# Crowded experts: one loop over blocks of 32 slots in place of nested written-out blocks

## The chip, the cores and the metric

The kernel runs on one core of a Trainium2 chip. The metric is device time in microseconds of one execution, from a median of runs.

## The reference, cut to what matters

One layer: a token mixer (retention and an mLSTM side by side) and then a mixture of experts over 512 tokens with 1024 features. Each token goes to one of 4 groups and there to 2 of 8 experts, so 1024 assignments are spread over 32 experts. What an expert gets depends on the data.

```python
def expert_block(args):
    xb, e = args
    return (jax.nn.silu(xb @ w_e1[e]) * (xb @ w_e3[e])) @ w_e2[e]
...
xs = u[slot_tok].reshape(n_blocks, MOE_BLOCK, D)
ys = lax.map(expert_block, (xs, block_exp)).reshape(n_slots, D)
out = jnp.zeros((N, D), F32).at[slot_tok].add(slot_w[:, None] * ys)
```

The weights `w_e1` and `w_e3` are 1024 x 512 and `w_e2` 512 x 1024 in float32, so an expert has three matrices of 2 MB.

## The kernel before, in words

The stages ahead of the experts (modulation, projections, scans, branches, routing) take the first 995 us or so of the span and are not touched. The routing leaves, in SBUF, for each expert the number of blocks of 32 slots that it fills (`nblk`), a row in the output scratch `y_d` (`orow`), and for each token its rank in its expert (`rm`).

The experts run in order, in one written-out Python loop (32 copies of the code). The order of the instructions on TensorE is the order of the source there (a manual schedule); the other engines are ordered by the scheduler. Copies of the weights go through a ring of ten 2 MB slots; SyncE issues the three loads of a later expert after each expert's code (L936). For expert e:

- `nb = values_load` (L1561) reads the next expert's count into a register of every engine.
- `hidden_q` for slots 0 to 31: 64 matmuls of 32 slots by 256 columns (L1464), their gate on ScalarE and VectorE (`swiglu`, L1445 to L1447).
- If n >= 2 (L1567): the same for slots 32 to 63.
- Every fourth expert: `gather`, which picks the rows of the next four experts with one-hot matmuls (L1424).
- `output_q`: two transposes (L1454), their copy (L1456), the output product (L1475, 32 matmuls in the trace), a product with the gate on VectorE (L1477), and a store on ScalarE's queue.
- `slots_in`: VectorE copies the next expert's slots from PSUM to `xT` (L1432).
- If n >= 2 (L1577): output of the second block and its store (L1579). Inside it, if n > 2 (L1580): `several`, the crowded path.

`several` before: `more` builds the one-hot of 64 slots (`osb`, L1482, against `rme`, L1496), gathers them with 96 matmuls (L1488) and copies them, half on ScalarE (L1490), half on VectorE (L1491). `some` runs `hidden_q` and `output_q` for 32 of them and stores the result in four DMAs of 32 KB from GpSimd (L1505). `some(1, ...)` stands in its own If, n > 3 (L1509); then n > 4 (L1511) with a second `more`, n > 5 (L1514), n > 6 (L1516), and in that a loop for n from 6 on (L1518). For the two blocks of one `more` there are two halves of `yq`, and so the first product of the second block can run while the first block's result is stored.

Of the 32 experts, 21 have n of 0 or 1, 8 have n = 2, two (25 and 28) have n = 3 and one (24) has n = 5, as the branches in the trace show.

## Time and profile before

| what | us |
|---|---|
| median of three runs | 1705.09 |
| lowest and highest of them | 1703.87, 1715.65 |
| the profiled execution | 1702.87 |
| its span, first to last instruction | 1700.9 |

The profile is one execution taken by the hardware profiler. PE is TensorE's matmuls, PEld its weight loads, DVE is VectorE, ACT ScalarE, POOL GpSimd, SP SyncE; a q behind the name is the engine's sequencer, which runs branches, waits and register loads. A wait is idle time of an engine in front of an instruction, put down to what came last. PEclk is the granted clock of TensorE as a share of its full speed. Weights (LDWEIGHTS) and matmuls of one product are separate instructions. The rows that matter stand in the section on rows.

### The profile page before, as it was taken

What the parts mean: (1) busy time and instruction counts of PE and PEld (TensorE: products, weight loads), DVE (VectorE), ACT (ScalarE), POOL (GpSimd) and SP (SyncE); (2) the same over time, 40 slices, a digit from 0 to 9 for tenths busy, and PEclk for the clock granted to TensorE, in tenths of its full rate; (3) what the DMA queues carried; (4) which work ended last, traced back from release to release, by engine and by line L of the source; (5) the groups of instructions that cost most, each with busy time, mean ns of one, the idle gap of its engine ahead of it and who ended that gap; (6) DMA issues with size and microseconds to landing.
All of it is one profiled execution on the core that took longest, in us unless ns stands there. A gap on an engine that the chain in (4) does not pass through costs nothing. (4 is left out here: it accounts for less than half of the span.)

```text
span 1700.9 us, 29095 instructions
## 1 busy us (share of the span) xinstructions
PE 1405.3 (83%) x11759; PEld 1101.2 (65%) x11759; DVE 785.4 (46%) x1893; ACT 426.1 (25%) x768; POOL 184.6 (11%) x113
## 2 busy tenths in 40 slices
PE   5999898999999999999999656576657676777774
PEld 3888888888898989899887544243434343444431
DVE  7747386567546475657687951111111111111115
ACT  3422254334444444445341210000000000000001
POOL 0101063235000000000132420000000000000003
PEclk9999999999999999999999778788878887998987
DMA  9324964344322122214557758889797979447544
GB/s 350 118 77 148 304 194 145 106 143 137 82 69 69 51 83 67 69 56 149 184 176 267 297 215 334 319 346 392 305 354 285 355 295 394 189 164 286 212 167 152
DMA packets 155875, 344.63 MB, mean 203 GB/s; under 512 B 18152, under 2 KB 110712, under 8 KB 147396
## 3 DMA queue, kind: packets, MB, share of 16 engines
q1 hardware_dynamic: 147544, 328.38, 53.2%
q10 hardware_dynamic: 6252, 7.73, 1.4%
q0 software_dynamic: 1792, 4.85, 0.8%
q8 instruction: 160, 2.62, 0.6%
q14 instruction: 127, 1.04, 0.2%
HBM read 307.37 MB, written 33.57 MB: 200 GB/s over the span
## 5 line engine op out<-in xcount | busy, mean ns | idle before, releaser
L1464 PE MATMUL ps_h<-w,xT 128*32 128x256 f32 x3072 | 241.2, 479 | 143.8 <-PEq L1561 96.0
L1464 PEld LDWEIGHTS ps_h<-w,xT 128*32 128x32 f32 x3072 | 131.8, 136 | 253.3 <-issue 199.1
L1446 DVE SCALAR_TENSOR_TENSOR t<-t,ps_h 64x256 f32<-64x256 f32 x48 | 19.8, 413 | 293.2 <-ACT t L1445 293.1
L187 DVE TENSOR_TENSOR w_lo<-raw,w_hi 128x1024 fp32r<-128x1024 f32 x96 | 127.2, 1348 | 23.6 <-ACT w_hi L186 23.6
L1445 ACT ACTIVATE t<-ps_h 64x256 f32<-64x256 f32 x48 | 17.7, 376 | 455.7 <-PE ps_h L1464 440.1
L1475 PE MATMUL ps_y<-w,hT 128*32 128x256 f32 x1536 | 104.7, 418 | 19.6 <-ACT hT L1456 11.9
L186 ACT ACTIVATE w_hi<-raw 128x1024 fp32r<-128x1024 f32 x96 | 96.1, 1050 | 60.3 <-PE ps_t L207 18.0
L550 POOL TENSOR_TENSOR macc<-macc,mw 128x1024 f32<-128x1024 f32 x32 | 81.5, 2546 | 97.3 <-DMA macc<-in_b_ada_dram 48.6
L1432 DVE COPY xT<-xg 128x128 f32<-128x128 f32 (+1 forms) x120 | 30.0, 295 | 125.9 <-PE xg L1424 65.6
L1475 PEld LDWEIGHTS ps_y<-w,hT 128*32 128x32 f32 x1536 | 49.0, 117 | 55.9 <-ACT hT L1456 15.9
L1424 PE MATMUL xg<-sg,u 128*128 128x256 bf16 (+1 forms) x768 | 80.5, 266 | 2.1 <-PEq L1567 1.2
L206 PE MATMUL ps_q<-u_lat,w_hi 128*128 128x512 f32 x192 | 78.4, 408 | 2.4 <-ACT u_lat L312 1.7
L1424 PEld LDWEIGHTS <-u 128*128 128x128 bf16 x768 | 70.5, 98 | 13.8 <-issue 6.4
L207 PE MATMUL ps_q<-u_lat,w_hi 128*128 128x512 f32 x192 | 77.9, 406 | 0.2 <-DVE u_lat L313 0.2
L208 PE MATMUL ps_q<-u_lat,w_lo 128*128 128x512 f32 x192 | 77.8, 405 | 0.0
L1505 POOL DMA_DIRECT2D y_d<-yq x20 | 10.2, 510 | 613.3 <-DVE yq L1477 500.7
L206 PE MATMUL ps_g<-w_hi,u_lat 128*128 128x256 f32 x256 | 72.6, 284 | 0.0
L208 PE MATMUL ps_g<-w_hi,u_lat 128*128 128x256 f32 x256 | 72.6, 284 | 0.0
L207 PE MATMUL ps_g<-w_lo,u_lat 128*128 128x256 f32 x256 | 72.5, 283 | 0.0
L206 PE MATMUL ps_v<-w_hi,u_lat 128*128 128x256 f32 x256 | 72.1, 282 | 0.0
L207 PE MATMUL ps_v<-w_lo,u_lat 128*128 128x256 f32 x256 | 72.1, 282 | 0.0
L208 PE MATMUL ps_v<-w_hi,u_lat 128*128 128x256 f32 x256 | 72.1, 282 | 0.0
(394 smaller groups left out, 3384.6 us busy)
## 6 DMA issues: line engine op xcount, KB each, us to landing
w<-in_w_e_dram SPq DMA_DIRECT2D x96, 2048.0 KB
raw<-in_w_in_dram SPq DMA_DIRECT2D x40, 1024.0 KB
mw<-in_w_ada_dram SPq DMA_DIRECT2D x32, 512.0 KB
y_d<-plain SPq DMA_DIRECT2D x28, 512.0 KB
wada<-in_w_ada_dram SPq DMA_DIRECT2D x4, 2048.0 KB
y_d<-yt ACTq DMA_DIRECT2D x43, 128.0 KB
tanh_d<-tg SPq DMA_DIRECT2D x16, 256.0 KB
br_d<-rt SPq DMA_DIRECT2D x16, 256.0 KB
```

The source lines that it names most:

```text
L186: S.activation(h_, r_, AF.Copy)
L187: V.tensor_sub(l_, r_, f32(h_))
L206: PE.matmul(ps, lh, rh, start=first, stop=False)
L207: PE.matmul(ps, lh, rl, start=False, stop=False)
L208: PE.matmul(ps, ll, rh, start=False, stop=last)
L550: G.tensor_add(acc, acc, w)
L1424: PE.matmul(xg[j // step][:, j % step], u2[s_][:, i, j * P:(j + 1) * P], sg[:, i], start=(i == 0 and s_ == 0), stop=(i == 3 and s_ == 2))
L1432: V.tensor_copy(xT[:, j:j + step, :], xg[j // step][:, :, n, :])
L1445: S.activation(t, ps[0:64, 0:256], AF.Tanh, scale=0.5)
L1446: V.scalar_tensor_tensor(t, t, 1.0, ps[0:64, 0:256], op0=OP.add, op1=OP.mult)
L1464: PE.matmul(ps[32 * a:32 * a + 32, 0:256], x[:, kt, 32 * b:32 * b + 32], w[a // 2][:, kt, 256 * (a % 2):256 * (a % 2) + 256], start=(kt == ...
L1475: PE.matmul(py[32 * a:32 * a + 32, 0:256], hT[:, kt % 2, 32 * (kt // 2):32 * (kt // 2) + 32], w2[:, kt, 256 * a:256 * a + 256], start=(kt ...
```

## The change

`several` becomes one loop that runs once for each block of 32 slots from the third on: the offset of the ranks falls by 32, `more` gathers 32 slots in place of 64 into the first half of `xT` (VectorE alone copies), and one block runs and is stored. The nested Ifs, their copies of the block and the hidden loop behind them are gone; so are the two halves of `yq`.

```diff
-    rme = m1p.tile([P, 4, 2], F32, name="rme")
+    rme = m1p.tile([P, 4, 1], F32, name="rme")
...
-        S.copy(xT[:, 0:4], ps[:, 0:4])
-        V.tensor_copy(xT[:, 4:8], ps[:, 4:8])
+        V.tensor_copy(xT[:, :, 0:32], ps)
...
     def several(e, w, n, xT, yq):
 
-        for b in range(2):
-            V.tensor_scalar(rme[:, :, b:b + 1], rm[:, :, e:e + 1], -64.0 * (b + 1), None, op0=OP.add)
-
+        V.tensor_scalar(rme, rm[:, :, e:e + 1], -32.0, None, op0=OP.add)
         base = nc.values_load(orow[0:1, e:e + 1], min_val=64 * NE, max_val=64 * NE + 1024)
-
-        def some(b, row):
-
-            y = yq[:, b, :]
-            output_q(hidden_q(xT, w, b), w[2], y)
+        with tc.For_i(2, n) as i:
+            V.tensor_scalar(rme, rme, -32.0, None, op0=OP.add)
+            more(xT)
+            output_q(hidden_q(xT, w, 0, gated("t")), w[2], yq)
             for a in range(4):
-                stored(G.dma_start(y_d[bass.ds(row, 32), 256 * a:256 * a + 256], y[32 * a:32 * a + 32, :]))
-
-        more(0, xT)
-        some(0, base)
-        with tc.If(n > 3, label=f"more{e}d"):
-            some(1, base + 32)
-            with tc.If(n > 4):
-                more(1, xT)
-                some(0, base + 64)
-                with tc.If(n > 5):
-                    some(1, base + 96)
-                    with tc.If(n > 6):
-                        V.tensor_scalar(rme, rme, -64.0, None, op0=OP.add)
-                        with tc.For_i(6, n, 2) as i:
-                            V.tensor_scalar(rme, rme, -64.0, None, op0=OP.add)
-                            more(0, xT)
-                            for b in range(2):
-                                some(b, base + i * 32 - 64 + 32 * b)
+                stored(G.dma_start(y_d[bass.ds(base + i * 32 - 64, 32), 256 * a:256 * a + 256], yq[32 * a:32 * a + 32, :]))
```

The lines of the new kernel are some 22 lower: the first If of an expert is L1545, the second L1555, the crowded path's L1558, and the loop L1495.

On PE, in the code of expert 0 of before, the second block's output ends and the crowded path begins with its first `more` (`ps_or` is its PSUM tile, `u` one of the three parts of the tokens):

```order
5672 L1475 MATMUL ps_y<-w_10040,hT 32x256 x16
5673 L1577 COMPARE_AND_BRANCH
5674 L1454 MATMUL ps_ht<-small,t_10118 128x64 x2
5675 L1475 MATMUL ps_y<-w_10040,hT 32x256 x16
5676 L1580 COMPARE_AND_BRANCH
5677 L1488 LDWEIGHTS u_9126
```

In the new program the crowded path stands at the same place (row 5676), but other rows follow it, as below. This is where the crowded path of before ends, behind its inner loop, with the ends of the nested Ifs, and the next expert begins:

```order
6367 L1475 MATMUL ps_y<-w_10040,hT 32x256 x16
6368 L1518 REGISTER_ALU
6369 L1518 COMPARE_AND_BRANCH
6370 L1518 UNCONDITIONAL_BRANCH
6371 L1516 UNCONDITIONAL_BRANCH
6372 L1514 UNCONDITIONAL_BRANCH
6373 L1511 UNCONDITIONAL_BRANCH
6374 L1509 UNCONDITIONAL_BRANCH
6375 L1580 UNCONDITIONAL_BRANCH
6376 L1577 UNCONDITIONAL_BRANCH x2
6377 L1561 TENSOR_LOAD nblk
```

Rows 5677 to 6375 are what an expert with n = 2 jumps over. A float32 matmul of these rows is two weight loads and two matmuls on the engine, so these rows are 1796 instructions, and 1870 with the second block's output.

In the new program PE has at the same place the entry of the loop, with a compare of its own and a block of its own in front of the body:

```order
5672 L1474 MATMUL ps_y<-w_10040,hT 32x256 x16
5673 L1555 COMPARE_AND_BRANCH
5674 L1453 MATMUL ps_ht<-small,t_10118 128x64 x2
5675 L1474 MATMUL ps_y<-w_10040,hT 32x256 x16
5676 L1558 COMPARE_AND_BRANCH
5677 L1495 COMPARE_AND_BRANCH
5678 L1495 UNCONDITIONAL_BRANCH x2
5679 L1656 BRANCH_PREFETCH_HINT
5680 L1487 LDWEIGHTS u_9126
5681 L1487 MATMUL ps_or<-osb,u_9126 128x32
```

Three branch rows and a hint have come in front of the gather; the gather's matmuls are 32 columns wide. The end of the body, and of the crowded path, on PE in the new program; the next expert follows:

```order
5889 L1474 MATMUL ps_y<-w_10040,hT 32x256 x16
5890 L1495 REGISTER_ALU
5891 L1495 COMPARE_AND_BRANCH
5892 L1495 UNCONDITIONAL_BRANCH
5893 L1558 UNCONDITIONAL_BRANCH
5894 L1555 UNCONDITIONAL_BRANCH x2
5895 L1539 TENSOR_LOAD nblk
5896 L1463 MATMUL ps_h<-w_10042,xT 32x256 x2
5897 L1463 MATMUL ps_h<-w_10044,xT 32x256 x2
```

The next expert begins 482 rows earlier: the crowded path's 700 rows are some 217, and four of its Ifs are gone. Its instructions are 413 in place of 1796, 487 in place of 1870 with the second block's output.

On SyncE in the new program, with the semaphores that a row waits for as far as they are printed: the entry, the way back to the loop's head, the start of the body, and the way out. DMASW are the semaphores of GpSimd's DMAs, DMAHW of the other queues.

```order
244 L1495 COMPARE_AND_BRANCH
245 L1495 UNCONDITIONAL_BRANCH
246 L1495 UNCONDITIONAL_BRANCH [waits DMASW2_49,DMASW1_49,DMASW3_49,DMASW0_49,DMAHW0_49,SP_sequencer_49,DMAHW1_49,DVE_sequencer_49,DMAHW2_49,PE_sequencer_49,DMAHW3_49,Activation_sequencer_49,DMAHW4_49,Pool_sequencer_49,DMAHW5_49,DVE_49,DMAH
247 L1656 BRANCH_PREFETCH_HINT
248 L1495 REGISTER_ALU
249 L1495 COMPARE_AND_BRANCH
250 L1495 UNCONDITIONAL_BRANCH [waits DMASW3_49,DMASW2_49,DMAHW0_49,DMASW1_49,DMAHW1_49,DMASW0_49,DMAHW2_49,SP_sequencer_49,DMAHW3_49,DVE_sequencer_49,DMAHW4_49,PE_sequencer_49,DMAHW5_49,Activation_sequencer_49,DMAHW6_49,Pool_sequencer_49,D
251 L1558 UNCONDITIONAL_BRANCH [waits SP_sequencer_49]
```

SyncE had no such rows on the path that runs in before, where the Ifs alone stand there; both the way back and the way out wait for the landings of all DMAs, and PE's way out (its row L1495 UNCONDITIONAL_BRANCH at the end of the body) waits for the same list.

## Rows read from the trace of the kernel before

**Rows 1.** The page's 40 slices of the span, PE, in tenths.
```profile
PE   5999898999999999999999656576657676777774
```

**Rows 2.** Waits, 980 to 1700.9 us: who waited for whom, us in total, times, longest.
```profile
PE ps_h L1464 <- PEq L1561: 96.0, 21, 7.1
...
PE ps_h L1464 <- DVE xT L1432: 35.1, 9, 6.0
...
DVE yt L1477 <- DMA w<-in_w_e_dram: 10.0, 3, 4.4
...
PE ps_h L1464 <- issue: 7.9, 7, 1.8
```

**Rows 3.** Stretches: us; PE, PEld, DVE, ACT, POOL busy (count); PEclk, DMA share, GB/s.
```profile
995.00:1440.00 445.00, 295.35 (x3490) 174.27 (x3489) 70.75 (x219) 18.82 (x59) 0.00 (x0) 0.81 0.84 333
...
1471.00:1508.00 37.00, 25.16 (x492) 16.03 (x490) 6.80 (x20) 2.71 (x8) 6.15 (x12) 0.95 0.12 35
1508.00:1525.00 17.00, 14.75 (x196) 8.25 (x196) 2.10 (x5) 1.24 (x4) 0.06 (x1) 0.80 0.92 370
...
1541.00:1597.30 56.30, 43.97 (x586) 28.23 (x585) 7.93 (x22) 3.08 (x10) 0.36 (x1) 0.92 0.85 338
...
1407.60:1414.10 6.50, 1.50 (x28) 0.66 (x20) 0.42 (x1) 0.00 (x0) 0.00 (x0) 0.97 1.05 432
1577.70:1581.60 3.90, 1.49 (x28) 0.65 (x20) 0.42 (x1) 0.00 (x0) 0.00 (x0) 1.00 0.06 12
...
1414.90:1421.50 6.60, 6.27 (x64) 3.26 (x64) 0.35 (x2) 0.02 (x1) 0.00 (x0) 0.58 0.90 323
```

**Rows 4.** PE's sequencer at the branches, 980 to 1700.9 us: ns min/median/max.
```profile
L1567 PEldq COMPARE_BRANCH  x43: 74/196/444, 998.8 to 1650.0; - x43
L1577 PEldq COMPARE_BRANCH  x43: 64/187/7497, 1002.7 to 1656.5; - x43
L1580 PEldq COMPARE_BRANCH  x11: 68/3895/6202, 1169.2 to 1630.3; - x11
L1509 PEldq COMPARE_BRANCH  x5: 65/181/3612, 1481.8 to 1611.8; - x5
L1514 PEldq COMPARE_BRANCH  x2: 181/1828/3475, 1503.2 to 1506.9; - x2
```

**Rows 5.** DMA queues, 995 to 1660 us: packets, MB, share.
```profile
q8 instruction: 112, 1.84, 1.1%
```

**Rows 6.** Timeline: start, length, engine, line, [idle before <- releaser].
```profile
1415.14 6.27 PE L1464 MATMUL ps_h<-w,xT 128*32 128x256 f32 x64 [6.04 <-PEq L1561]
...
1472.11 2.96 PE L1488 MATMUL ps_or<-osb,u 128*128 128x64 bf16 x96 [1.07 <-DVE osb L1482]
1475.53 3.66 PE L1464 MATMUL ps_h<-w,xT 128*32 128x256 f32 x64 [0.46 <-ACT xT L1490]
...
1481.36 3.14 PE L1475 MATMUL ps_y<-w,hT 128*32 128x256 f32 x32 [0.37 <-ACT hT L1456]
1484.25 4.18 PE L1464 MATMUL ps_h<-w,xT 128*32 128x256 f32 x64
...
1485.29 2.30 POOL L1505 DMA_DIRECT2D y_d<-yq  x4 [495.00 <-DVE yq L1477]
...
1502.71 1.93 PE L1475 MATMUL ps_y<-w,hT 128*32 128x256 f32 x32 [0.37 <-ACTq L1514]
1507.99 1.02 PE L1464 MATMUL ps_h<-w,xT 128*32 128x256 f32 x11 [3.34 <-DVE xT L1432]
...
1540.87 4.50 PE L1464 MATMUL ps_h<-w,xT 128*32 128x256 f32 x40 [2.88 <-DVE xT L1432]
...
1612.88 3.64 PE L1464 MATMUL ps_h<-w,xT 128*32 128x256 f32 x32 [2.10 <-DVE xT L1432]
```

**Rows 7.** GpSimd's stores of the crowded blocks, L1505, ns min/median/max.
```profile
L1505 POOL DMA_DIRECT2D y_d<-yq x20: 496/496/736, 1485.3 to 1613.3; - x20
...
DMA to landing us min/median/max: 1.7/3.8/7.5
```

## Prediction, made before the changed kernel was run

> **What bounds the kernel now.** I read the page first: TensorE (PE) is busy 9 tenths or nearly so in the first 22 of the 40 slices, and 4 to 7 tenths in the last 18, in which the experts run [rows 1]. Then the waits: PE's first matmul of an expert (L1464) waited 96.0 us in 21 gaps that end at PE's own sequencer, and 35.1 us in 9 gaps that end at VectorE's copy of the slots, while the only wait for expert weights is 10.0 us in 3 cases, on VectorE [rows 2]. So the stage is bound by PE's chain, though not by much: from 995 to 1440 us the weights came at 333 GB/s with the DMA engines busy 0.84, and where they come fastest it is 370 GB/s at 0.92 [rows 3].

> Only three experts run the path. The stores of L1505 are 20, four to a block, so 5 blocks of 32 slots run [rows 7]: three in expert 24 (1471 to 1508), one in expert 25 (1525 to 1541), one in expert 28 (1597.3 to 1613). Hardly a weight is in flight there, the DMA share over expert 24 is 0.12 [rows 3] and alike in the other two, so every microsecond of their PE chain is on the path to the end.

> **The change part by part.** Part A, less code. Rows of PE's order fall from 30,887 to 15,463, and the jump over the crowded path from 1870 to 487 instructions (L1555) and from 1796 to 413 (L1558). Does a shorter jump cost less? The nested branches of before answer: L1514 jumps 811 instructions in 3.5 us and L1509 1403 in 3.6 us, both with the DMA engines nearly idle, against 3.9 us for 1796 [rows 4]. A fetch costs the same whatever is skipped, until the target is already there, as for 128 instructions. 413 and 487 exceed one 256-instruction piece, so by the instruction counts 25 of the 29 jumps still land past the piece that follows; 4 land in it, just asked for, and I give these 0 to 1 us each, 1 us together. A second saving: those seven second stops come where a landing is close to the end of a piece. With the new positions I count about half of it, 4 us. Part A: -5 us. Its ends: 0 (all landings equally bad), and the first rival's gain.

> [...]

> Part B, the block alone. Of the 13.46 us of expert 24's first block (1471.04 to the end of its output at 1484.50), 1.07 is the wait for the one-hot, 2.96 the gather of 64 columns, 0.46 the copy, 3.66 the first product, 2.17 the gate on ScalarE and VectorE, the transposes and their copy (1479.19 to 1481.36), and 3.14 the output [rows 6]. The new gather has 96 matmuls of 32 columns. The trace has none of that shape; by columns it would be half, 1.5 us, by weight loads (one for each matmul) still 2.96. I take 12.4 us for a block behind its one-hot: what the shorter gather gives is taken again by a clock that falls in the longer pause before it, as at 1415.14.

> Part C, what is no longer shared or overlapped. Before, two blocks share one gather, and the second one's first product starts at 1484.25 while the first one's output is being stored: the second and third together, with one more gather, end 20.1 us after the first (1504.64) [rows 6]. After, each block has its gather and starts behind the loop's edge.

> Part D, the edges. In the built program the way back to the loop's head and the way out wait, on SyncE and by a barrier on all engines, or on each engine itself, for every semaphore, those of the four GpSimd stores' landings among them. From the trace: the output ends at 1484.50, the first store issues at 1485.29, four take 2.30 us [rows 6], so the last is issued some 1.8 us after the first, and a store lands at the soonest 1.7 us after its issue [rows 7]: 0.8 + 1.8 + 1.7 = 4.3 us to the last landing. Nothing in the trace shows the wait itself. For the way out I add 1.2 us for some ten waits in a row on PE's sequencer and 1.0 us for branches and the load of the next block count: 6.5 us. For the way back, 0.6 us of waits on SyncE, 1.4 us for two barrier rounds and 0.7 us for new rank offsets and the one-hot: 7.0 us. These small figures are my choices. Their lower end: the gaps stay what they were, 1.07 us between blocks and 3.34, 2.88 and 2.10 us on the way out [rows 6]. Upper end: a code fetch of 3.5 us that only starts behind the wait is added at each of the five edges. I stand between, since the stores' landing is measured and the fetch can run beside it. The longest landing is 7.5 us [rows 7], but that is under weights in flight, which the loops do not have: the ring is full before they start.

> What is queued behind: GpSimd has nothing else; SyncE's next weight loads stand behind the loop, as they stood behind the nested path, into a ring that is full by then, so they start later by as much as PE does; VectorE's copies of the next expert's slots wait too, and PE's next product for them, which is in the 1.0 us.

> Sum. Expert 24: 13.46 + 2 x (7.0 + 12.4) + 6.5 = 58.8 us against 36.95 (1471.04 to 1507.99): +21.8. Expert 25: 6.5 - 2.88 = +3.6. Expert 28: 6.5 - 2.10 = +4.4. Together +29.8; with Part A +24.8. On the profiled execution of 1702.87 us (span 1700.9 and 2.0 around it) this gives 1728 us; that execution lies 2.2 us under the median of 1705.09, within the spread of the three. With the lower end of the edges expert 24 takes 13.46 + 2 x (1.07 + 12.4) + 3.34 = 43.7, +6.8 in all, and 1705 us; with the upper end +29.8 + 5 x 3.5 - 5 = +42 and 1745 us.

> **The rivals.** First, on the other side: the shorter jump finds its code there. PE's gaps at an expert's start would go, at most 96.0 + 35.1 us [rows 2]. But then the weights bind: what came in 445 us at 333 GB/s takes 400 us at 370 GB/s, and the 56.3 us from 1541 take some 51, so 50 us is the most. With +30 for the crowded experts that is 1683 us, faster by 1.2%. For it: the 0.2 us of L1567. Against it: the stall is the same for 811 instructions as for 1796, and a jump of 413 leaves its piece as one of 811 does. It decides from a window on of 500 instructions ahead of the branch. 5%.

> [...]

> Second, cheap edges: the landings are not waited for in earnest, or the barrier costs what an ordinary semaphore does. Then the gap between blocks is some 2 us (the 1.07 of before and the branches and barriers), the ways out stay as they were, and little more than the lost sharing is paid: 6.8 + 2 x 0.9 - 5 = +3.6, about 1707 us, no change. For it: a store's landing takes only 1.7 us. Against: the program's waits name the store semaphores. 22%.

> Third, dear edges: on each way back and out PE fetches code only after the wait, or waits are slower than I think, 3.5 us more at five edges: 1745 us. [...] Against: the fetch can begin at the branch, and each body begins with a prefetch hint. 12%.

> The forecast has 61%, its own range 1718 to 1738.

> **How the numbers follow.** A measurement of this kernel can tell about 1%, 17 us. Slower by more: most of the forecast (0.55), all of the third (0.12), and a little of the second: 0.68. Within: the rest of the forecast and most of the second: 0.27. Faster by more: the first, 0.05. For 8 in 10 the range reaches down to the lower end of the edges, 1705, leaving out the first rival and a part of the second, and up to 1748, just past the upper end.

> **What would show it.** In the changed kernel's branches: L1555 and L1558 still 3.3 to 7.5 us in most of 29 cases (right), or all near 0.2 us (first rival). In the timeline of expert 24: three blocks with 6 to 8 us of idle PE after each output (right), 2 us (second), over 9 us (third), with the landing of the stores just before PE goes on. Expert 24 should take 55 to 62 us from its one-hot to the next expert's first matmul. Packets on the instruction queue in the expert stage should fall from 112 [rows 5] by only a few. The prediction is wrong if the crowded three together lose less than 15 us, or if the other 29 experts change by more than 15 us.

## The result, and the profile after

The changed kernel takes 1725.34 us (median of six, 1721.68 to 1734.98); beside it the kernel before had 1707.36 us. The ratio is 1.0111, 95% interval 1.0069 to 1.0154: slower by 18 to 19 us, where 1728 us was forecast. The profiled execution took 1725.59 us with a span of 1723.9. That is 22.7 us more than the profiled execution of before, whose 1702.87 us lie under the median of its kernel.

The sequencer's rows for TensorE (PE) at the three Ifs of an expert in the changed kernel, ns min/median/max; L1545, L1555 and L1558 answer to L1567, L1577 and L1580 of [rows 4]:

```profile
L1545 PEldq COMPARE_BRANCH  x43: 67/201/2813, 1001.1 to 1675.6; - x43
...
L1555 PEldq COMPARE_BRANCH  x43: 64/2198/7020, 1005.0 to 1682.1; - x43
...
L1558 PEldq COMPARE_BRANCH  x11: 68/3956/5922, 1171.9 to 1656.4; - x11
```

The jumps skip 487 and 413 instructions in place of 1870 and 1796 and cost what they did: L1558 has a median of 3.96 us where L1580 had 3.90, and its eight far jumps sum to 38.0 us against 38.2. The 21 far jumps at L1555 sum to 105.5 us against 105.6 at L1577. (The median of L1555 is one way out of the loop that has moved to the middle of the 43.) The two L1545 branches of 2.8 and 1.7 us I read as second stops that now fall on a branch.

PE's timeline over the crowded path of expert 24, and the first matmuls after the paths of experts 25 and 28 (start, length, what it is, [idle before <- releaser]); it answers to [rows 6]:

```profile
1468.61 2.56 PE L1487 MATMUL ps_or<-osb,u 128*128 128x32 bf16 x96 [1.26 <-DVE osb L1481]
1471.69 4.96 PE L1463 MATMUL ps_h<-w,xT 128*32 128x256 f32 x64 [0.52 <-DVE xT L1489]
...
1478.92 1.93 PE L1474 MATMUL ps_y<-w,hT 128*32 128x256 f32 x32 [0.43 <-ACT hT L1455]
1487.49 2.72 PE L1487 MATMUL ps_or<-osb,u 128*128 128x32 bf16 x96 [6.64 <-DVE osb L1481]
1490.73 3.99 PE L1463 MATMUL ps_h<-w,xT 128*32 128x256 f32 x64 [0.52 <-DVE xT L1489]
...
1506.03 2.72 PE L1487 MATMUL ps_or<-osb,u 128*128 128x32 bf16 x96 [6.60 <-DVE osb L1481]
...
1516.48 1.93 PE L1474 MATMUL ps_y<-w,hT 128*32 128x256 f32 x32 [0.43 <-ACT hT L1455]
1527.26 8.12 PE L1463 MATMUL ps_h<-w,xT 128*32 128x256 f32 x99 [8.85 <-PEq L1539]
...
1562.72 2.79 PE L1463 MATMUL ps_h<-w,xT 128*32 128x256 f32 x24 [6.78 <-DMA y_d<-yt]
...
1641.19 4.22 PE L1463 MATMUL ps_h<-w,xT 128*32 128x256 f32 x37 [6.76 <-DMA y_d<-yt]
```

The numbers in brackets are the loop: 6.64 and 6.60 us of idle PE on the two ways back, 8.85, 6.78 and 6.76 us on the three ways out. Each names a different releaser (VectorE's one-hot, PE's own sequencer, a store), since the edge waits for everything and the last in line gets the name. Expert 24 takes 59.9 us from the end of the output before its path (1467.35, which is 1468.61 less the 1.26 of idle time) to the next expert's first product, where it took 36.95.

What the edge is made of stands in the rows of the loop's own line and of the stores in it, here for the first way back, 1484 to 1488 us:

```profile
L1495 SPq EVENT_SEMAPHORE  x12: 17/28/28, 1484.8 to 1486.8; - x12
...
L1495 PEldq EVENT_SEMAPHORE  x3: 51/51/51, 1486.3 to 1486.8; - x3
```

```profile
L1500 POOL DMA_DIRECT2D y_d<-yq x4: 496/516/733, 1481.7 to 1483.7; - x4
...
DMA to landing us min/median/max: 1.7/1.8/1.9
```

The output ends at 1480.85. GpSimd issues the last of four stores at 1483.7; a landing takes 1.7 to 1.9 us, which is 1485.5. SyncE, which began its waits at 1484.8, goes through a dozen of them, the other engines' two rounds end at 1486.8, and PE's gather starts at 1487.49.

Weights: from 995 to 1395 us they came at 332 GB/s (331 before); the instruction queue moved 106 packets from 995 to 1680 us, where before it moved 112 up to 1660 us, by which time that kernel was as far along.

```profile
995.00:1395.00 400.00, 267.70 (x3243) 163.42 (x3240) 67.97 (x218) 17.19 (x54) 0.00 (x0) 0.84 0.85 332
```

```profile
q8 instruction: 106, 1.74, 1.0%
```

### The profile page after: what moved, and what is told of

It is laid out like the page before. It is cut to its first block, busy times and chain, and to the rows that moved or that the text cites. A ratio compares the mean times of both kernels' runs of the same rounds, so it can differ in the third digit from the quotient of the medians.

```text
span 1723.9 us, 29503 instructions
## 1 busy us (share of the span) xinstructions
PE 1405.2 (82%) x11855; PEld 1101.0 (64%) x11855; DVE 785.1 (46%) x1897; ACT 424.5 (25%) x764; POOL 184.4 (11%) x113
## 5 line engine op out<-in xcount | busy, mean ns | idle before, releaser
L186 DVE TENSOR_TENSOR w_lo<-raw,w_hi 128x1024 fp32r<-128x1024 f32 x96 | 126.8, 1344 | 22.7 <-ACT w_hi L185 22.7
L1474 PE MATMUL ps_y<-w,hT 128*32 128x256 f32 x1536 | 100.8, 405 | 20.5 <-ACT hT L1455 10.3
```

The source lines that it names most:

```text
L186: V.tensor_sub(l_, r_, f32(h_))
L1474: PE.matmul(py[32 * a:32 * a + 32, 0:256], hT[:, kt % 2, 32 * (kt // 2):32 * (kt // 2) + 32], w2[:, kt, 256 * a:256 * a + 256], start=(kt ...
```

## The experiments

Two questions are open behind a time that came out as forecast. Are the edges dear because of the landings, or because of barriers or the lost sharing? And did the 29 other experts gain (some 9 us by the profile) because the code is shorter? Ratios are to the kernel before, timed in turn with each on the same chip.

**1. The same blocks without a loop.**

```diff
-        with tc.For_i(2, n) as i:
-            V.tensor_scalar(rme, rme, -32.0, None, op0=OP.add)
-            more(xT)
...
+        block(base)
+        with tc.If(n > 3):
+            block(base + 32)
+            with tc.If(n > 4):
+                block(base + 64)
+                with tc.If(n > 5):
+                    with tc.For_i(5, n) as i:
+                        block(base + i * 32 - 64)
```

> The changed kernel's blocks of 32 slots, each with its own gather, but written out in nested Ifs instead of the loop (the loop is left only for a sixth block on, which no expert has). Theory (the loop's edges cost the time, because they wait for the landing of the stores and pass two barriers): the gaps of 6.6 us between blocks of expert 24 fall to 1.1 to 1.4 us, the ways out from 8.9, 6.8 and 6.8 us to 2 to 3.5, expert 24 takes some 43 us from its first gather to the next expert's first product, and the time is 1705 to 1713 us. Rival (what is lost is the shared gather and the overlap of two blocks): the time stays near 1725, expert 24 over 52 us.

Measured: 1699.79 us, ratio 0.9952 (0.9926 to 0.9977). PE's timeline at the second and third gather of expert 24 and at the first products after the three paths:

```profile
1472.13 2.74 PE L1487 MATMUL ps_or<-osb,u 128*128 128x32 bf16 x96 [0.93 <-DVE osb L1481]
...
1484.62 2.56 PE L1487 MATMUL ps_or<-osb,u 128*128 128x32 bf16 x96 [0.95 <-DVE osb L1481]
...
1498.36 6.90 PE L1463 MATMUL ps_h<-w,xT 128*32 128x256 f32 x118 [1.21 <-DVEq L1507]
...
1529.69 2.36 PE L1463 MATMUL ps_h<-w,xT 128*32 128x256 f32 x38 [3.12 <-DVE xT L1431]
...
1604.26 1.06 PE L1463 MATMUL ps_h<-w,xT 128*32 128x256 f32 x15 [2.25 <-DVE xT L1431]
```

The gaps fall to 0.93 and 0.95 us, the ways out to 1.21, 3.12 and 2.25. Expert 24 takes 39.9 us (1458.45 to 1498.36), 3.0 more than before. So lost sharing and overlap are worth 3 us, the loop's edges 20 of the 23 us that expert 24 lost. The time is under the expected range: the lost sharing had been put at 6.8 us, and the other experts came out better than before, of which more below. (The profiled execution, of 1690.83 us, is the fastest of the eight.)

**2. A short path without a loop.** `several` ends after `some(0, base)`; everything behind it is taken out.

> The kernel before with only the first crowded block; the second and third block of expert 24 are left out. The jump over the path is as short as in the changed kernel, without a loop. Theory (shorter code moves landings but the jumps still fetch code): the branches at L1577 and L1580 still take 3.3 to 7.5 us in most of 29 experts, the 31 experts besides number 24 change by -10 to 0 us together, expert 24 loses 20 us, and the time is 1677 to 1690 us. Rival (a shorter jump finds its code there): the 31 experts lose up to 50 us, 1635 to 1655 us.

Measured: 1655.10 us, 0.968 (0.9644 to 0.9717), between the two. The rows of the two branches in it (ns min/median/max):

```profile
L1563 PEldq COMPARE_BRANCH  x43: 64/191/7081, 1004.1 to 1619.1; - x43
```

```profile
L1566 PEldq COMPARE_BRANCH  x14: 67/3334/5645, 1167.1 to 1593.5; - x14
```

The jumps cost what they did, so the rival's mechanism is not there. Of the 54 us, 23.5 are the two blocks and the way out of expert 24 (36.95 less 13.46; PE goes on there without a gap), and 5.0 are the idle 2.88 and 2.10 us at the ends of experts 25 and 28, where the far branch of 3.6 and 3.4 us is gone. The rest, some 26 us by the medians, is more than the -10 to 0 expected. The profiled execution, the slowest of the five, shows 14 us less of it. What made up this part was not settled.

**3. The stores behind the loop.** Only the last block of an expert is stored, so 12 stores run in place of 20.

```diff
             output_q(hidden_q(xT, w, 0, gated("t")), w[2], yq)
-            for a in range(4):
-                stored(G.dma_start(y_d[bass.ds(base + i * 32 - 64, 32), 256 * a:256 * a + 256], yq[32 * a:32 * a + 32, :]))
+        for a in range(4):
+            stored(G.dma_start(y_d[bass.ds(base, 32), 256 * a:256 * a + 256], yq[32 * a:32 * a + 32, :]))
```

> The changed kernel with the four stores behind the loop instead of in it: only the last block of an expert is stored, at the place of the first; the rows of the other crowded blocks are left out. Theory (the edge is 4.6 us to the landing of the last store and 2.0 us of waits, barriers and one-hot): the two gaps between blocks of expert 24 fall from 6.6 to 2.5 to 3.2 us, each way out from 8.9, 6.8 and 6.8 by 3 to 4.5 us, and the time by 16 to 21 us, to 1704 to 1710. Rival (waits and barriers are the price, whatever is stored): gaps stay over 5 us, the time over 1718.

Measured: 1701.59 us, 0.9968 (0.9937 to 0.9999). PE's timeline at the same five places:

```profile
1480.69 2.66 PE L1487 MATMUL ps_or<-osb,u 128*128 128x32 bf16 x96 [2.14 <-DVE osb L1481]
...
1494.44 2.67 PE L1487 MATMUL ps_or<-osb,u 128*128 128x32 bf16 x96 [2.13 <-DVE osb L1481]
...
1510.21 9.86 PE L1463 MATMUL ps_h<-w,xT 128*32 128x256 f32 x128 [4.20 <-issue]
...
1540.82 4.49 PE L1463 MATMUL ps_h<-w,xT 128*32 128x256 f32 x40 [1.88 <-issue]
...
1612.22 4.05 PE L1463 MATMUL ps_h<-w,xT 128*32 128x256 f32 x48 [1.88 <-issue]
```

All five edges fall by 4.5 to 4.9 us, the ways out by a little more than expected, and the time is just under the expected range. A way back is 4.5 us of stores and 2.1 us of waits, barriers and one-hot. Of the 1725 us of the changed kernel some 23 (five edges) hang on stores whose data nobody in the loop reads.

**4. The other way to make the loop's edge cheap.**

```diff
-        with tc.For_i(2, n) as i:
+        with tc.For_i(2, n, iteration_sync="staggered") as i:
```

> The changed kernel with the loop's semaphores reset a stage at a time while the body runs, in place of the barrier at the way back. Theory (the way back costs 6.6 us because it waits for the landing of the stores and for two barriers): the two gaps between blocks of expert 24 fall to 1.5 to 4 us, the ways out stay at 6 to 9, and the time falls by 5 to 10 us, to 1713 to 1721. Rival (the landings are waited for in any case): 1723 to 1728.

Measured: 1727.69 us, 1.0104 (1.0071 to 1.0138). PE's timeline at the first two blocks of expert 24, the third gather, and the way out:

```profile
1471.66 6.20 PE L1463 MATMUL ps_h<-w,xT 128*32 128x256 f32 x64 [1.39 <-DVE xT L1489]
...
1485.85 0.90 PE L1487 MATMUL ps_or<-osb,u 128*128 128x32 bf16 x30 [3.85 <-DVE osb L1481]
...
1490.20 5.47 PE L1463 MATMUL ps_h<-w,xT 128*32 128x256 f32 x64 [1.08 <-DVE xT L1489]
...
1503.62 0.96 PE L1487 MATMUL ps_or<-osb,u 128*128 128x32 bf16 x30 [3.81 <-DVE osb L1481]
...
1525.14 10.01 PE L1463 MATMUL ps_h<-w,xT 128*32 128x256 f32 x128 [4.86 <-issue]
```

The ways back fall to 3.85 and 3.81 us as expected, and the way out falls to 4.86 us, where it was expected to stay. The time does not fall: it misses the theory's range and lies in the rival's, though the edges did get shorter. What the edges gave, the body took. The three blocks, from a gather's start to the end of its output, take 45.0 us together where they took 36.6, the first of them too, which has no way back in front of it. The second block's first product takes 5.47 us where it took 3.99, and its copy keeps PE waiting 1.08 us in place of 0.52. The mean granted clock over the whole path is 0.76 in both kernels. Over the blocks alone it is 0.77, 0.77 and 0.62 against 0.87, 0.76 and 0.77, so the first and the third also ran at a lower clock; the second is 2 us longer at the same clock. Why was not settled. The path takes 59.3 us (1465.88 to 1525.14) against 59.9. An edge that is cut from 6.6 to 3.8 us in this way is worth nothing here; one that is gone, as in the first experiment, is.

**5. Does the length of the skipped code matter?** Two kernels in which nothing that runs is changed but the length (in the second also one branch more for the three crowded experts). First the kernel before without its innermost loop (blocks from the seventh on are left out; no expert has them):

> The kernel before without its innermost If and the loop in it (blocks from the seventh on, which no expert has here): nothing that runs changes, the jump over the crowded path gets some 600 instructions shorter and every landing moves. Theory (what a shorter path gives without a loop is only where the landings fall): the 32 far branches stay at 3.3 to 7.5 us each and the time stays within 12 us of before, either way. Rival (the length itself costs): 15 to 30 us faster.

Measured: 1703.13 us, 0.9966 (0.9945 to 0.9988), some 5 us faster. Then the changed kernel with three blocks that nobody enters:

```diff
+        with tc.If(n > 15):
+            for b in range(3):
+                V.tensor_scalar(rme, rme, -32.0, None, op0=OP.add)
+                more(xT)
...
```

> The changed kernel with three written-out blocks behind its loop in an If that no expert enters (n over 15): the jump over the crowded path is again some 1600 instructions, nothing that runs is added but one branch for the three crowded experts. Theory (29 jumps cost the same at 487 instructions as at 1870; what the other experts gained is where the landings fall): apart from up to 3 x 3.5 us for the new far jump behind the loop, the time stays within 10 us of the changed kernel's, 1717 to 1745 us, and 29 jumps sum to 135 to 155 us in the trace. Rival (the shorter code gave the other experts their 7 to 14 us): these are lost again, and the padded kernel is 17 to 25 us slower than the changed one, 1742 to 1750.

Measured: 1746.13 us, 1.0238 (1.0197 to 1.0279). By the time alone the rival is right. The trace says where more than half of the 21 us went: the wait before the next expert's first product after the paths of experts 24, 25 and 28, behind the new jump (L1501).

```profile
1527.12 8.12 PE L1463 MATMUL ps_h<-w,xT 128*32 128x256 f32 x116 [11.59 <-DVE xT L1431]
```

```profile
1566.51 5.87 PE L1463 MATMUL ps_h<-w,xT 128*32 128x256 f32 x59 [12.24 <-DVE xT L1431]
```

```profile
1656.03 9.16 PE L1463 MATMUL ps_h<-w,xT 128*32 128x256 f32 x128 [11.34 <-DMA y_d<-yq]
```

```profile
L1501 PEldq COMPARE_BRANCH  x6: 186/2121/4717, 1521.7 to 1655.0; - x6
```

These gaps are 2.7, 5.5 and 4.6 us longer than in the changed kernel, 12.8 us together; the new jump takes 4.3, 4.7 and 4.1 us. Another 8.5 us are spread over the work behind expert 24's path. Part of them is a lower clock: the two outputs of expert 28 ahead of its path (1622.7 to 1631.8) take 3.64 us each at a mean granted clock of 0.50, where they took 1.93 at 1.00. What brought that clock down was not tested. The 29 jumps of the other experts sum to 149.5 us, as the theory said. The experts ahead of expert 24 lost nothing. PE's time from its first load of a block count to the load with which expert 24 begins, by the traces (the start of that instruction, twice):

| kernel | instructions skipped at the first far branch | us | sum of the rest, to the end |
|---|---|---|---|
| before | 1870 | 462.0 | 245.2 |
| before, without inner loop | some 1270 | 463.4 | 247.0 |
| changed | 487 | 455.2 | 273.2 |
| changed, padded | some 1600 | 451.8 | 294.5 |
| written out | some 1600 | 446.3 | 246.1 |
| short path | some 470 | 453.3 | 211.9 |
| stores behind the loop | 487 | 453.8 | 249.0 |

There is no order by length in the third column: the two with some 1600 instructions are the fastest. Each row is one execution, and executions of one kernel lie 10 to 25 us apart here (that of the written-out kernel is the fastest of its eight). So the 6.8 us that the 24 experts gained in the changed kernel are not told apart from that spread, nor put down to the length or the position of the code. By the time the theory's range was missed by 1 us; by the place of the loss it holds for the experts ahead of expert 24, while the 8.5 us behind it stay open.

**6. Asking for the code in time.** The two far branches of an expert are announced to PE's sequencer ahead of time; if the stall is a fetch, it should then be shorter.

```diff
+            tc.mark_branch_hint_location(f"more{e}b", n >= 2, engines=[EN.PE])
             t0 = hidden_q(xT, w, 0, gated("t0"))
...
-            with tc.If(n >= 2):
+            with tc.If(n >= 2, label=f"more{e}b"):
+                tc.mark_branch_hint_location(f"more{e}c", "LikelyTaken", engines=[EN.PE])
                 output_q(t1, w[2], yt[:, 256:512])
...
-                with tc.If(n > 2):
+                with tc.If(n > 2, label=f"more{e}c"):
                     several(e, w, n, xT, yq)
```

> The changed kernel with a prefetch hint on TensorE: at the start of each expert for the branch over the second block's output (by the value of n), and at the start of that output for the branch over the crowded path. Theory (a far jump is a fetch of code that nobody asked for in time): the two branches fall from 3.3 to 7.0 us to under 1 us in most of 29 experts, and the weights become the bound, so 20 to 50 us are gained, 1675 to 1705 us. Rival (the fetched piece is thrown out before the branch, or the stall is something else): branches as before, 1725 us.

Measured: 1676.01 us, 0.9791 (0.9745 to 0.9837). The branches of over 1 us on PE fall from 32 with 150.2 us in sum to 19 with 74.0 us, and the weights now come almost without a pause. The expectation held for the time; of the branches it held for fewer than half, since 17 of the 29 far jumps still take over 1 us.

```profile
995.00:1395.00 400.00, 287.68 (x3565) 176.38 (x3565) 73.78 (x240) 19.40 (x63) 0.00 (x0) 0.86 0.96 374
```

Announced, these branches cost half of what they did (74.0 us of 150.2), as they should if the stall is a fetch. The weights now move at 374 GB/s with a DMA share of 0.96, so there is little room left, as the first rival of the prediction had it for its own case. That they bind is read from this share: PE's own waits for a weight's landing are 2.2 us of these 400. The branch at L1560 (n = 2), announced only at the start of the output, kept its stall:

```profile
L1560 PEldq COMPARE_BRANCH  x11: 77/4928/6329, 1134.6 to 1615.8; - x11
```

Is early better? The first hint moved to just ahead of `output_q(t0, ...)`:

> The hinted loop with the first of its two hints moved from the start of the expert to the start of the first block's output, some 68 TensorE instructions ahead of the branch in place of 200 to 390. Theory (a hinted piece is kept only until the next piece is fetched, and an early hint is lost when TensorE runs over an edge of a piece): the far branches over 3 us at the second block's output fall from 4 to 0 to 2, those between 1 and 3 us grow, since a fetch under the weights takes longer than the output; the time stays within 8 us of 1676, as the weights bind. Rival (earlier is better): over 10 branches above 3 us there, 1685 us or more.

Measured: 1709.99 us, 1.0026 (1.0000 to 1.0052), against my theory: 27 branches are over 1 us with 125.4 us in sum, and 13 of those at the second block's output over 3 us, where it was 4. A hint 68 instructions ahead of the branch leaves most of the stall here, 125.4 us of 150.2.

```profile
L1556 PEldq COMPARE_BRANCH  x43: 67/195/7170, 1002.4 to 1664.6; - x43
```

**7. The best of it.** Written out, the first hint at the start of the expert, the second one at the start of the second block's first product:

> The written-out blocks of 32 of the first experiment, with prefetch hints on TensorE: for the branch over the second block's output at the start of the expert, by the value of n; for the branch over the crowded path at the start of the second block's first product, earlier than in the hinted loop. Theory (loop edges and code fetches are separate losses): the loop's share of about 25 us comes off the 1676 us of the hinted loop, 1645 to 1662 us, with the weights at 370 GB/s or more up to expert 24. Rival (the weights bind everywhere and hide the loop's edges): within 8 us of 1676.

Measured: 1641.85 us, 0.9624 (0.9586 to 0.9662), the fastest kernel here, 65 us under before. The time is just under the expected range; the weights came at 365 GB/s from 995 to 1395 us, a little under the 370 expected. The earlier second hint works (L1569, n = 2):

```profile
L1569 PEldq COMPARE_BRANCH  x11: 77/376/6407, 1147.7 to 1573.6; - x11
```

The same hints in the kernel before:

> The kernel before with the same hints, its crowded path unchanged. Theory (a hint takes the target's piece early, however far it is): far branches over 3 us fall from 32 to under 12, 1645 to 1665 us. Rival (the jump of 1800 instructions is dearer to hint than one of 400): over 1675 us.

Measured: 1648.28 us, 0.9654 (0.9602 to 0.9706). 12 of its PE branches are still over 3 us, one more than the most expected, and the time is where it was expected: that jumps of 1870 and 1796 instructions are dearer to announce (over 1675 us) is not what this run shows. The intervals of the two kernels overlap.

## Why the prediction was right

- **What bounds.** The wait at an expert's start is the far jump: shown by the hints, which halve what these branches take (150.2 to 74.0 us) and bring 49 us (1725 to 1676). That the jump is a fetch of code fits this and the equal price of 487 and 1870 skipped instructions (105.5 and 105.6 us for the 21 jumps).
- **Part A, -5 us.** The jumps cost the same, as argued: shown by the rows above and by the padded kernel. The size came out near (the experts ahead of expert 24 took 6.8 us less) and its reason did not, so that was luck. I had put it on landings counted in the new code, 4 us of second stops and 1 us of near jumps. No jump became near: all 29 take 3.3 us or more. Second stops did not fall either: 0.75, 0.34, and the 2.8 and 1.7 at L1545 make 5.6 us, and one of 4.0 us stands behind a first weight load, 9.6 in all against 7.9. What gave the 6.8 us stays open.

```profile
1088.49 0.20 PEld L1463 LDWEIGHTS ps_h<-w,xT 128*32 128x32 f32 x7 [3.97 <-issue]
```

- **Part B, 12.4 us a block.** Measured from a gather's start to the end of its output: 12.24 (1468.61 to 1480.85), 11.93 for the second and 12.38 for the third (1506.03 to 1518.41). The gather of 32 columns takes 2.56 to 2.72 us, near the upper of the two bounds, 2.96: its 96 weight loads stay, and half the columns save little. As forecast, the first product takes that back or more: 4.96, 3.99 and 4.95 us against 3.66, the first of them at a mean granted clock of 0.72 (1471 to 1477).
- **Part C.** The lost sharing was worth 3.0 us, as experiment 1 shows, and not the 6.8 of the lower end.
- **Part D, the edges.** 6.64 and 6.60 us on the way back against 7.0; 6.78 and 6.76 on two of the ways out against 6.5. The landing is the larger part, 4.5 us by experiment 3 (4.3 worked out). The third way out, 8.85, was mis-sized by 2.3: behind the waits PE's jump to the next expert takes 2.2 us (the median of L1555, from 1524.5 us on). Without the stores this way out is longer than the other two by the same 2.3 us (4.20 against 1.88). I read it as the third rival's fetch behind the wait, at one of five edges in place of all; why there alone was not tested.
- **Sum.** Expert 24: +22.9 (59.9 less 36.95) against +21.8. Experts 25 and 28, ways out: +3.9 and +4.7 against +3.6 and +4.4. That is 31.5 against 29.8; the span grew by 23.0, so all else gave 8.5 back where 5 was forecast. How near 1728 us came also hangs on its starting point, the profiled execution: by the medians the change costs 18 us and not 22.7, less than the 24.8 forecast. The second rival's cheap edges exist, but only where the body stores nothing (2.1 us).

## What to carry to other kernels

This loop, whose turns are few and short, pays for each turn, and for leaving it, the landing of what its body has just stored plus a fixed sum: on the way back 4.5 and 2.1 us against 12 us of work. Blocks written out in nested Ifs cost neither here (0.93 and 0.95 us between blocks), and no cost of the added code's length was found once the jump over it was far anyway. In another kernel with such a loop both are worth a measurement. Announcing the far jumps ahead of time brought 49 us here, and then the DMA engines that bring the weights are busy 0.96; what it brings elsewhere hangs on what binds next.

## What the runs showed that was not expected

A hint 68 instructions ahead of its branch left 125 us of far branches, one at the start of the expert 74 us. Over the 24 experts ahead of the crowded ones, kernels that skip other lengths of code differ by some 17 us (446.3 to 463.4), one execution each, with no order by length. A loop with its semaphores reset in stages cut the ways back from 6.6 to 3.8 us and left the time as it was, because the blocks themselves got slower (45.0 us for three where they took 36.6).
